# SBUF tiles of a four-layer network placed at multiples of 512 bytes

## The chip, the cores and the metric

The kernel runs on one core of a Trainium2 chip. A time is the device time of one execution in microseconds (us); what is compared is the median over several executions of a program. A profiled execution also leaves a trace, in which each instruction has its engine, its start and its duration. The core has five engines that work side by side: TensorE (PE, with its weight loads shown apart as PEld), VectorE (DVE), ScalarE (ACT), GpSimd (POOL) and SyncE (SP), whose queue starts most transfers. Operands lie in SBUF, the on-chip memory of 128 partitions; an address here is the number of bytes from the start of a partition, the same on every partition a tile uses.

## The reference

One sequence of 512 tokens with 1,024 features goes through four layers, all in float32: two of a first block, one of a second, one of a third. Each layer has a mixer and a feed-forward network with a hidden width of 2,816. What counts for the change is that every layer is a row of large products with weights from HBM, and that three mixers hold a running sum of log decays along the tokens, started anew at the first token of each chunk. Cut down:

```python
def first_block(x, c, ...):                     # layers 0 and 1, gated by a modulation silu(c) @ ada_w + ada_b
    x = x + gate * norm(mixer_ssd_mla(h(x)))    # layer 0: state-space scan (SSD) beside latent attention
    x = x + gate * norm(swiglu(h(x)))
    x = x + gate * norm(mixer_gla_nsa(h(x)))    # layer 1: gated linear attention beside sparse attention
    x = x + gate * norm(swiglu(h(x)))

def second_block(x, ...):                       # dilated attention, two convolution branches, feed-forward

def third_block(x, ...):                        # RWKV-7 beside gated DeltaNet, feed-forward
    u = rms_norm_3(x, norm1_g); p = u @ w_in
    ...
    h = causal_depthwise_conv_3(rms_norm_3(x, norm2_g) @ ffn_up, ffn_conv_w)
    x = x + (silu(h_gate) * h_up) @ ffn_down
    return rms_norm_3(x, final_g)

# the running sums of decays, within each chunk:
#   SSD:       a_cs = cumsum(dt * a)        over chunks of 128 tokens, 16 heads
#   GLA:       bc = cumsum(log_a)           over chunks of tokens, 4 heads of 128 features
#   DeltaNet:  gc = cumsum(g)               over chunks of tokens, 4 heads
```

## The kernel before

**Products.** Activations are kept by feature: a tile [128 features, 512 tokens], 2,048 bytes a partition. A float32 product is made in three passes of float32r parts: weights and activations are split into a high and a low part, and `mm3` (L246 on) issues high by high, high by low, low by high into one PSUM bank. Its two operands are the weights (128x128, the stationary tile: `whi` or `wlo`) and the activations (128x512, the moving tile: `h`, the input of a layer, or `s`, a slot of a phase). All of its matmuls are recorded at line L248. `gemm_tok` (L334) makes products by token the other way round: the activations are stationary, 128 tokens at a time, and up to 512 columns of weights move (L349 to L351).

**Weights.** `wtiles` (L222) takes at most 8 blocks of 128x128: one transfer of 512 KB on SyncE's queue into `wraw`, then `split` (L360) makes `whi` on ScalarE (L364) and `wlo` on VectorE (L365). A tile of 8 blocks serves 24 matmuls. A scheduler of priorities sets the order on each engine; what a mixer computes besides its products (small two-pass float32 matmuls at L824, L837, L844 among them) is traced with steps so that products fill the gaps between.

**Memory.** Four pools that last for the whole program are laid one behind the other in this order: `cpool` (constants `cst` and `vec`), `wpool` (`wraw`, `whi`, `wlo`), `tpool` (small tiles and temporaries `ta`, `tb`, `td`), `hpool` (eight slots of 4,096 bytes for `h`). Behind them lies a pool of the phase, with slots `s` of 4,096 bytes, which each phase opens anew. Each tile is rounded up to 32 bytes only, so the size of the constants decides where all others begin: `wraw`, `whi` and `wlo` start at 128 past a multiple of 512, the `h` slots at 320 past one, and so do the slots of all phases but one. In the mixer of block 3 (`b3_mixer`, L1656 on), two tiles of constants lie ahead of the slots, which puts these at 384.

**Running sums.** `rst128` is a constant of 512 columns in `cst`, 1 everywhere but at the first column of each 128. A scan computes, column by column, constant times the running value plus the next element, so one scan of 512 columns does four chunks of 128. There are six: one for layer 0 (L993 in `l0_ssd`, 16 partitions), four for layer 1 (L1315 in `gla_decays`, one for each head), one for block 3 (L1998 in `gdn_decays`, 4 partitions):

```python
nc.vector.tensor_tensor_scan(bs(hd), self.c("rst128"), e, 0.0, ALU.mult, ALU.add)
```

Of the kernel before, what the change touches and what calls it, by code (L numbers as in the profile page):

```python
# [26 lines left out]
# order of the work: priorities and steps between what runs side by side, slots and tiles of the phases  # L27
# [21 lines left out]
class Core:  # L49
    """Helpers shared by the layers: weight streaming, float32 products in three passes of float32r  # L50
    parts, norms over features. Activations by feature live in slots of 4 KB a partition."""

    def __init__(self, ctx, tc, a, offs):
# [4 lines left out]
        self.pp = pool("pp", space=PSUM)  # L58
        self.hslots = [None] * 8
# [19 lines left out]
    def consts(self, group, t=None, queue=None):  # L79
        """Load a group of constants, not before the instruction of self.mark has been issued."""  # L80
        if t is None:
            t = self.s4([128, self.a[group].shape[1]])
        if self.mark is None:
            (queue or self.nc.scalar).dma_start(t, self.a[group])
        else:
            with self.tc.issue_after(self.mark.ins):
                self.nc.scalar.dma_start(t, self.a[group])
        self.groups[group] = t
# [12 lines left out]
    # ---- memory: tiles of one tag are handed out in the order traced, so streams of work that are to  # L101
    # run side by side have tags of their own
    @contextmanager
    def psum(self, **banks):
        """The banks of the streams a and b, for the phases in the block."""
# [31 lines left out]
    def s4(self, shape=(128, 2, T), dt=F32, tag="s4"):  # L137
        """A slot of 4 KB a partition of the phase."""
        return self.spool.tile(list(shape), dt, tag=tag, name=self.nm(tag), bufs=self.nslots[tag] if isinstance(self.nslots, dict) else self.nslots)

    def fa(self, dt=F32, tag="s4"):
        """Tiles of features [128, T], two to a slot, taken when first used."""
# [11 lines left out]
    def h4(self, i, dt=F32):  # L154
        """Slot i % 8 (two tiles of features) of the memory of the input of a layer, free for float32, or for
        float32r parts, in place of those before."""
# [6 lines left out]
    def ha(self, slots, dt=F32):  # L163
        """As fa, in slots of the input of a layer."""
# [11 lines left out]
    def parts(self, tag="s4"):  # L176
        """Tiles of features as float32r parts: x(k) = (high, low). Tag h: the input of a layer."""
# [9 lines left out]
    def later(self, by):  # L187
        """What the block traces yields to what is traced up to `by` instructions after it."""
# [6 lines left out]
    def paced(self, by):  # L195
        """Products traced in the block, and what belongs to them, run between what is traced after it: a step
        of 3 passes every `by` instructions."""
# [10 lines left out]
    def beside(self):  # L208
        """What the block traces has the priority of what is traced after it."""
# [4 lines left out]
    def step(self, at):  # L214
        """The priority of one step of paced products, counted from at."""
# [6 lines left out]
    def wtiles(self, src, blocks):  # L222
        """At most 8 blocks [128, 128] of weights, as float32r parts [128, 1024]."""
# [12 lines left out]
    def wload(self, w, m0, nm, k0, nk):  # L236
        """m-tiles m0.. and k-tiles k0.. of a packed weight [m, 128, k, 128], as float32r parts: nm times a
        function of k."""
# [15 lines left out]
    def gemm(self, w, x, evac, m0=0, nm=None, wide=False, tail=0):  # L254
        """For each m-tile of packed w: evac(m, PSUM [128, T]) of w^T x; x(k) gives float32r parts, to be
        scaled by token after the product if there is x.rows. Wide: 4 m-tiles at first, for tiles of x that
        become ready one after the other, or 3 by halves of the tokens where x does. Tail: the last m-tiles
        by halves of the tokens, with evac(m, PSUM of the half, its slice)."""
# [22 lines left out]
    def gemm_tail(self, w, x, evac, m0, n):  # L281
        """At most 24 blocks of weights, loaded once. What follows the first half runs under the second."""
# [19 lines left out]
    def gemm_wide(self, w, x, evac, m0, n):  # L302
# [5 lines left out]
        for half in halves:  # L308
            for k in range(nk):
# [3 lines left out]
                for m in range(n):  # L313
                    # the first product of a bank clears it for both halves
# [19 lines left out]
    def gemm_tok(self, w, x, evac, n0=0, n=None):  # L334
        """By token: evac(j, PSUM [128, n]) of x^T w for the 4 tiles of tokens; w packed [128, k, N], n <= 512."""
# [24 lines left out]
    def split(self, hi, lo, src, scale=None):  # L360
        """hi + lo = src (times a per-partition scale), both float32r."""
# [10 lines left out]
    def sq_acc(self, acc, src, first, scale=1.0):  # L372
        """acc (+)= (src scale) squared."""
# [8 lines left out]
    def tok_sums(self, tiles, p=None, first=True, last=True):  # L382
        """[128, 4] by token in PSUM: sums over the partitions of all tiles. Not first: added to a bank with sums."""
# [6 lines left out]
    def pow_rstd(self, p, n, eps, pool=False):  # L390
        """(p / n + eps) ** -0.5 for a few columns p."""
# [8 lines left out]
        # Newton's method, from half the exponent: 3.5e-2, 2e-3, 5e-6, rounding  # L400
# [7 lines left out]
    def rstd_tok(self, tiles, n, eps=EPS, pool=False):  # L408
        """[128, 4] by token: (sum over partitions and tiles / n + eps) ** -0.5."""
        return self.pow_rstd(self.tok_sums(tiles), n, eps, pool)  # L410

    def bcast_tok(self, r):
        """[128, 4] by token -> PSUM [128, T], the same on every partition."""
        p = self.ps()
        self.bcast_to(p, r, 0)
        return p

    def bcast_to(self, p, r, j0):
        """[128, n] by token, of the tiles j0.. of tokens, into p."""
# [19 lines left out]
    def norm_h(self, r, x, gain, shift=None, update=None, h=None, half=slice(0, T)):  # L439
        """float32r parts of x rows gain (+ shift), by feature; r [128, T] the rows. update(k) completes x(k).  # L440
        With h: the half of the tokens of h."""
# [20 lines left out]
    def set_rows(self, h):  # L462
        """At the start of a phase: the factors by token that its input lacks, on all partitions."""
# [2068 lines left out]
```

## Time and profile before

| | us |
|---|---|
| median of 3 runs | 3778.25 |
| lowest and highest run | 3776.22, 3787.38 |
| span of the profiled execution | 3789.9 |
| TensorE busy in it | 3690.6 (97%) |
| weight loads (PEld, beside TensorE) | 2946.1 (78%) |
| VectorE busy | 2194.6 (58%) |
| ScalarE busy | 1357.0 (36%) |
| GpSimd busy | 242.3 (6%) |

The profiled execution is one of its own, with the time in the third line. A busy engine is one that has an instruction under way; matmuls are pipelined, so the duration of one overlaps the next, and the distance from one start to the next tells how fast they go. In a timeline a line of two instructions (x2) stands for both, with the start of the first and the end of the second. The granted clock (PEclk) is TensorE's clock as a share of 2.4 GHz, the upper of its two levels; 0.50 is the lower one, 1.2 GHz.

In order of time, the stages are: layer 0's mixer up to 471 us, its feed-forward to 841, layer 1's mixer to 1344, its feed-forward to 1714, block 2's mixer to 2384, its feed-forward to 2749, block 3's mixer to 3426, its feed-forward to 3761, and the last norm. "FFN" below means a feed-forward stretch.

### The profile page before, as it was taken

Reading aid. Unit: us, or ns where it says so; the run is one execution under the profiler, and the core shown is the slowest. Engines: PE = TensorE matmul, PEld = TensorE weight load, DVE = VectorE, ACT = ScalarE, POOL = GpSimd, SP = SyncE. Lnnn points to the kernel's source line nnn. Section 1 sums busy time; section 2 is a strip of 40 time slices with the busy share of each in tenths; the row PEclk is TensorE's granted clock in tenths of the full one; section 3 lists DMA queues with packets and bytes.
Section 4 is the critical chain, followed back from the end, with each engine's and each line's share of the span. In section 5 each row is a group of like instructions: output and inputs, shape, how many; then the busy total and the mean of one; then the engine's idle time right before and its main releaser. Section 6 shows DMA issues by size and latency. Waiting matters only on the chain.

```text
span 3789.9 us, 50851 instructions
## 1 busy us (share of the span) xinstructions
PE 3690.6 (97%) x20496; PEld 2946.1 (78%) x20496; DVE 2194.6 (58%) x3803; ACT 1357.0 (36%) x2197; POOL 242.3 (6%) x214
## 2 busy tenths in 40 slices
PE   7998999999999999999999999999999999999999
PEld 5776788877887778877878888788877777887887
DVE  7866655454377653338629354665466656766652
ACT  5344432324254432322332243443343332334432
POOL 2003100110022100101000010000000000100000
PEclk9998999999999999999989999999999999999999
DMA  6511265533310242333112234223321121152232
GB/s 217 181 47 56 99 201 188 167 111 98 119 31 23 66 152 94 117 95 103 57 39 73 84 102 138 90 95 116 93 98 40 61 69 43 32 178 89 95 117 73
DMA packets 120219, 373.75 MB, mean 99 GB/s; under 512 B 12064, under 2 KB 20128, under 8 KB 119984
## 3 DMA queue, kind: packets, MB, share of 16 engines
q1 hardware_dynamic: 105008, 322.05, 26.0%
q10 hardware_dynamic: 14976, 48.45, 3.8%
q8 instruction: 161, 2.64, 0.3%
q14 instruction: 74, 0.61, 0.1%
HBM read 349.49 MB, written 20.97 MB: 98 GB/s over the span
## 4 chain that ended last, share of the span: by engine, by line
PE 91%; DVE 6%; ACT 1%; issue 1%; DMA 0%; POOL 0%; POOLq 0%; DVEq 0%; ACTq 0%
PE pg L248 68%; PE pa L248 3%; PE pb L844 2%; PE pb L824 1%; PE pb L837 1%; PE pb L1264 1%; DVE wlo L365 1%; PE pa L387 1%; PE pg L1351 1%; PE pb L2264 1%; DVE wa L2142 1%; PE pg L349 0%; PE pa L349 0%; PE pa L350 0%; PE pg L350 0%
## 5 line engine op out<-in xcount | busy, mean ns | idle before, releaser
L248 PE MATMUL pg<-h,whi 128*128 128x512 f32 (+1 forms) x5584 | 1801.3, 401 | 44.8 <-ACT h L458 14.9
L248 PEld LDWEIGHTS pg<-h,whi 128*128 128x128 f32 x5584 | 1047.1, 190 | 307.3 <-ACT h L458 18.7
L248 PE MATMUL pg<-h,wlo 128*128 128x512 f32 (+1 forms) x2792 | 1113.4, 399 | 0.0
L364 ACT ACTIVATE whi<-wraw 128x1024 fp32r<-128x1024 f32 (+3 forms) x540 | 547.0, 1014 | 1414.7 <-PE pg L248 1106.1
L365 DVE TENSOR_TENSOR wlo<-wraw,whi 128x1024 fp32r<-128x1024 f32 (+3 forms) x540 | 639.2, 1185 | 665.2 <-ACT whi L364 662.4
L248 PE MATMUL pg<-s,whi 128*128 128x512 f32 (+1 forms) x2044 | 629.7, 390 | 2.6 <-DVE s L906 2.4
L248 PEld LDWEIGHTS pg<-h,wlo 128*128 128x128 f32 x2792 | 532.3, 191 | 123.5 <-issue 3.7
L248 PEld LDWEIGHTS pg<-s,whi 128*128 128x128 f32 x2044 | 379.1, 189 | 94.5 <-DVE s L906 3.7
L248 PE MATMUL pg<-s,wlo 128*128 128x512 f32 (+1 forms) x1022 | 397.3, 389 | 0.0
L248 PEld LDWEIGHTS pg<-s,wlo 128*128 128x128 f32 x1022 | 192.5, 188 | 43.5
L802 DVE SCALAR_TENSOR_TENSOR td<-td,vec,td 128x511 f32<-128x511 f32 (+1 forms) x188 | 139.9, 747 | 59.5 <-ACT td L798 57.9
L2142 DVE CUSTOM_DVE_ANT_0 wa<-wa,scb,vec 128x1024 f32<-128x1024 f32 x90 | 121.7, 1354 | 71.3 <-DMA wa<-in_l_ada_dram 71.2
L327 DVE TENSOR_TENSOR td<-pg,rows 128x512 f32<-128x512 f32 x130 | 89.7, 691 | 98.3 <-PE pg L248 98.0
L1500 DVE SCALAR_TENSOR_TENSOR s<-s,vec,s 128x504 f32<-128x504 f32 (+25 forms) x180 | 121.4, 731 | 0.4
L844 PEld LDWEIGHTS pb<-s,tb 128*128 128x128 f32 x600 | 83.6, 198 | 31.3 <-DVE tb L842 9.3
L248 PE MATMUL pa<-h,whi 128*128 128x512 f32 (+1 forms) x336 | 97.1, 363 | 0.0
L364 ACT ACTIVATE s<-td 128x512 fp32r<-128x512 f32 x94 | 59.3, 630 | 102.3 <-DVE td L489 102.0
L844 PE MATMUL pb<-s,tb 128*128 128x64 f32 x600 | 90.7, 281 | 2.9 <-DVE tb L842 2.9
L365 DVE TENSOR_TENSOR s<-td,s 128x512 fp32r<-128x512 f32 x94 | 66.9, 712 | 31.1 <-ACT s L364 31.1
L489 DVE TENSOR_TENSOR td<-td,pg 128x512 f32<-128x512 f32 x44 | 30.3, 688 | 80.9 <-PE pg L248 80.9
L248 PEld LDWEIGHTS pa<-h,whi 128*128 128x128 f32 x336 | 61.2, 194 | 10.1
L798 ACT ACTIVATE td<-td,vec 128x512 f32<-128x512 f32 x94 | 66.4, 708 | 4.5 <-DVE td L327 3.1
(804 smaller groups left out, 4140.4 us busy)
## 6 DMA issues: line engine op xcount, KB each, us to landing
wraw<-in_b_in_dram SPq DMA_DIRECT2D x112, 512.0 KB, 3.2
wraw<-in_l_up_dram SPq DMA_DIRECT2D x88, 512.0 KB, 3.2
wraw<-in_b_up_dram SPq DMA_DIRECT2D x88, 512.0 KB, 3.2
wa<-in_l_ada_dram ACTq DMA_DIRECT2D x80, 512.0 KB, 3.3
wraw<-in_l_in_dram SPq DMA_DIRECT2D x51, 512.0 KB, 3.3
wraw<-in_l_down_dram SPq DMA_DIRECT2D x32, 512.0 KB, 3.5
wraw<-in_b_down_dram SPq DMA_DIRECT2D x32, 512.0 KB, 3.5
xd<-s SPq DMA_DIRECT2D x28, 512.0 KB, 2.7
```

The lines of the kernel that those rows point to most:

```text
L248: mm = lambda *a, **k: self.nc.tensor.matmul(*a, **k, skip_group_check=True)
L327: self.nc.vector.tensor_mul(y, ps, rows)
L364: i = nc.scalar.activation(hi, src, AF.Copy)
L365: nc.vector.tensor_sub(lo, src, hi.bitcast(F32))
L387: self.pe_mark = self.nc.tensor.matmul(p[:, j : j + 1], t[:, j * 128 : j * 128 + 128], self.c("ones"), start=first and i + j == 0, stop=la ...
L798: nc.scalar.activation(out, ps, AF.Copy, scale=w(taps - 1))
L802: nc.vector.scalar_tensor_tensor(out[:, s:], ps[:, : T - s], w(taps - 1 - s), out[:, s:], ALU.mult, ALU.add)
L824: nc.tensor.matmul(s[:, :w], q, k, start=True, stop=True)
L837: nc.tensor.transpose(pt[:, b * 128 : b * 128 + 128], p[:, b * 128 : b * 128 + 128], self.ident)
L844: nc.tensor.matmul(o, st[:, b * 128 : b * 128 + 128], v(b), start=b == 0, stop=b == nb - 1)
L1500: nc.vector.scalar_tensor_tensor(out[:, s:], x[:, : T - s], tap(30 - s), out[:, s:], ALU.mult, ALU.add)
L2142: nc.vector.tensor_tensor_reduce(w, w, self.scb, 1.0, b, ALU.mult, ALU.add, o)
```

## The change

Two tiles that nothing reads are put at the ends of `cpool` and `tpool`, to fill the bytes up to the next multiple of 512. Each gets a memset of one column on GpSimd. To make room, `rst128` shrinks from 512 to 128 columns (`cst` from 788 to 404), and a scan of 512 columns becomes four of 128 in a new helper. In `b3_mixer` the two tiles of constants are rounded up to 128 columns, and a small tile grows from 80 to 128. Comments are dropped and line numbers shift by up to 11; all else is as it was.

```diff
+PADS = dict(cpool=384, tpool=320)
...
+        for n, size in PADS.items():
+            t = getattr(self, n).tile([128, size // 4], F32, name="pad")
+            nc.gpsimd.memset(t[:, :1], 0.0)
...
-    "rst128": _grid(lambda p, u: u % 128 != 0, 512),
+    "rst128": _grid(lambda p, u: u != 0, 128),
...
+    def scan128(self, out, x):
+
+        for t in (slice(c, c + 128) for c in range(0, T, 128)):
+            self.nc.vector.tensor_tensor_scan(out[:, t], self.c("rst128")[: x.shape[0]], x[:, t], 0.0, ALU.mult, ALU.add)
...
-        nc.vector.tensor_tensor_scan(cs, self.c("rst128")[:16], adt, 0.0, ALU.mult, ALU.add)
+        self.scan128(cs, adt)
...
-            nc.vector.tensor_tensor_scan(bs(hd), self.c("rst128"), e, 0.0, ALU.mult, ALU.add)
+            self.scan128(bs(hd), e)
...
         for g in ("cst3", "cst3b"):
-            self.consts(g, self.spool.tile([128, a[g].shape[1]], F32, name=g))
-        sm = self.small([128, 80], tag="b3", bufs=1)
+            n = a[g].shape[1]
+            self.consts(g, self.spool.tile([128, -(-n // 128) * 128], F32, name=g)[:, :n])
+        sm = self.small([128, 128], tag="b3", bufs=1)
...
-        nc.vector.tensor_tensor_scan(ab[:4], self.c("rst128")[:4], sp, 0.0, ALU.mult, ALU.add)
+        self.scan128(ab[:4], sp)
```

The start of each kind of tile, as bytes past a multiple of 512, in the two built programs:

| tile | before | after |
|---|---|---|
| `wraw`, `whi`, `wlo` | 128 | 0 |
| `h` slots | 320 | 0 |
| slots `s`, temporaries of a phase, block 3's mixer aside | 320 | 0 |
| slots `s` of block 3's mixer | 384 | 0 |

So the float32r matmuls with 512 columns come in these pairs of offsets (moving, stationary): before, 11,214 of (320, 128) at L248, 288 of (384, 128) at L248 in block 3, and 216 of (128, 320) in the product by token; after, all 11,718 of (0, 0).

On VectorE, before, the four scans of layer 1 stand right behind the operations that feed them (L1314); `s4_1159` and `s4_1164` are slots with two heads each, `ta` the temporaries, and a scan is printed as SCALAR_TENSOR_TENSOR:

```order
L1314 SCALAR_TENSOR_TENSOR ta_1158_6413<-s4_1159_6414,ta_1158_6413 128x512
L1314 SCALAR_TENSOR_TENSOR ta_1161_6420<-s4_1159_6414,ta_1161_6420 128x512
L1315 SCALAR_TENSOR_TENSOR s4_1159_6414<-cst_95,ta_1158_6413 128x512
L1315 SCALAR_TENSOR_TENSOR s4_1159_6414<-cst_95,ta_1161_6420 128x512
L1314 SCALAR_TENSOR_TENSOR ta_1163_6426<-s4_1164_6427,ta_1163_6426 128x512
```

And after, at the same place:

```order
L1324 SCALAR_TENSOR_TENSOR ta_1158_6420<-s4_1159_6421,ta_1158_6420 128x512
L1324 SCALAR_TENSOR_TENSOR ta_1161_6427<-s4_1159_6421,ta_1161_6427 128x512
L828 SCALAR_TENSOR_TENSOR s4_1159_6421<-cst_99,ta_1158_6420 128x128 x4
L828 SCALAR_TENSOR_TENSOR s4_1159_6421<-cst_99,ta_1161_6427 128x128 x4
L1324 SCALAR_TENSOR_TENSOR ta_1163_6433<-s4_1164_6434,ta_1163_6433 128x512
```

Each scan has become four in a row at its old place; nothing else has moved. At the start of GpSimd's queue, before, the memsets of the program's constants, the first of the kernel's own (`e`), and the first power of a norm:

```order
L2522 MEMSET const-bfloat16-1.0 128x1
L2522 MEMSET const-uint8-127 128x1
L2527 UNCONDITIONAL_BRANCH
L2226 MEMSET e_2641 128x8
L398 ISA
L398 TENSOR_TENSOR rya_131<-rxa_132,cst 128x4
```

And after:

```order
L2533 MEMSET const-bfloat16-1.0 128x1
L2533 MEMSET const-uint8-127 128x1
L2538 UNCONDITIONAL_BRANCH
L63 MEMSET pad 128x1 x2
L2237 MEMSET e_2648 128x8
L403 ISA
L403 TENSOR_TENSOR rya_135<-rxa_136,cst 128x4
```

The two memsets of the pads stand ahead of the kernel's first. On the other engines the rows are those of before but for a few neighbours of equal priority that change places.

## Rows read from the trace of the kernel before

**Rows 1.** Page, the chain that ended last, by engine and line; cores.

```profile
PE 91%; DVE 6%; ACT 1%; issue 1%; DMA 0%; POOL 0%; POOLq 0%; DVEq 0%; ACTq 0%
PE pg L248 68%; PE pa L248 3%; PE pb L844 2%; PE pb L824 1%; PE pb L837 1%; PE pb L1264 1%; DVE wlo L365 1%; PE pa L387 1%; PE pg L1351 1%; PE pb L2264 1%; DVE wa L2142 1%; PE pg L349 0%; PE pa L349 0%; PE pa L350 0%; PE pg L350 0%
...
core 0: 3789.9 us, clock 0.979
```

**Rows 2.** Groups by shape, TensorE: busy us, mean ns; idle before, releasers.

```profile
L248 PE MATMUL pg<-h,whi 128*128 128x512 f32 x5392 | 1763.3, 405 | 38.4 <-ACT h L458 11.7 <-DVE h L459 8.9 <-DVE td L327 5.9
L248 PE MATMUL pg<-h,wlo 128*128 128x512 f32 x2696 | 1087.1, 403 | 0.0
L248 PE MATMUL pg<-s,whi 128*128 128x512 f32 x1924 | 608.2, 397 | 2.6 <-DVE s L906 2.4 <-DVE s L802 0.2
L248 PE MATMUL pg<-s,wlo 128*128 128x512 f32 x962 | 380.7, 396 | 0.0
```

**Rows 3.** Timeline of TensorE, moving tile h: start, us, what.

```profile
3031.28 0.63 PE L248 MATMUL pg<-h,whi 128*128 128x512 f32 x2
3031.74 0.40 PE L248 MATMUL pg<-h,wlo 128*128 128x512 f32 x1
...
3035.48 0.63 PE L248 MATMUL pg<-h,whi 128*128 128x512 f32 x2
```

**Rows 4.** Timeline of TensorE, moving tile s of block 3.

```profile
3383.99 0.61 PE L248 MATMUL pg<-s,whi 128*128 128x512 f32 x2
3384.45 0.39 PE L248 MATMUL pg<-s,wlo 128*128 128x512 f32 x1
...
3388.07 0.61 PE L248 MATMUL pg<-s,whi 128*128 128x512 f32 x2
```

**Rows 5.** Timeline of TensorE, product by token.

```profile
980.41 0.39 PE L349 MATMUL pg<-whi,h 128*128 128x512 f32 x1
...
985.91 0.39 PE L349 MATMUL pg<-whi,h 128*128 128x512 f32 x1
```

**Rows 6.** Chain in 1891 to 1921, then that window's row.

```profile
1894.03 1.28 PE pg L248 x3
...
1891.00:1921.00 30.00, 30.00 (x88) 22.02 (x88) 4.62 (x25) 10.89 (x41) 0.00 (x0) 0.50 0.05 17
```

**Rows 7.** Windows: span, busy PE PEld DVE ACT POOL, PEclk, DMA share, GB/s.

```profile
128.00:471.00 343.00, 320.86 (x1761) 249.94 (x1759) 236.07 (x440) 144.14 (x270) 53.42 (x43) 0.94 0.27 89
471.00:841.00 370.00, 363.25 (x1545) 288.90 (x1545) 195.38 (x253) 112.15 (x147) 17.90 (x13) 0.99 0.51 166
...
1714.00:2384.00 670.00, 670.00 (x2955) 541.80 (x2956) 373.79 (x594) 219.71 (x404) 33.75 (x19) 0.96 0.26 85
...
2749.00:3426.00 677.00, 673.22 (x6340) 527.31 (x6339) 426.47 (x958) 226.47 (x381) 11.86 (x17) 0.99 0.23 74
```

**Rows 8.** Groups by shape, VectorE: whole span, 2384:2749, 2749:3426.

```profile
L365 DVE TENSOR_TENSOR wlo<-wraw,whi 128x1024 fp32r<-128x1024 f32 x460 | 570.2, 1241 | 571.0 <-ACT whi L364 568.4 <-PE pg L248 0.5 <-ACT sb L1803 0.4
...
L489 DVE TENSOR_TENSOR td<-td,td 128x512 f32<-128x512 f32 x22 | 15.1, 687 | 0.0
...
L2121 DVE TENSOR_TENSOR s<-s,s 128x512 f32<-128x512 f32 x4 | 2.7, 685 | 0.0
```

**Rows 9.** Chain at 96.91; line L1315; timeline at 14.93.

```profile
96.91 1.16 DVE s L993
...
L1315 DVE TENSOR_TENSOR_SCAN s<-cst,ta x4: 1200/1210/1220, 922.6 to 927.2; 128x512 f32<-128x512 f32 x4
...
14.93 0.16 DVE L396 TENSOR_SCALAR rxa<-pa 128x4 f32<-128x4 f32 x1 [1.96 <-PE pa L387]
```

**Rows 10.** Timeline of the first 20 us.

```profile
0.73 0.10 POOL L2226 MEMSET e<- 128x8 f32 x1 [0.29 <-POOLq L2522]
...
7.58 3.57 PE L387 MATMUL pa<-cst,sq 128*128 128x1 f32 x16 [7.58 <-DVE sq L2177]
...
15.17 1.01 POOL L398 TENSOR_TENSOR rya<-rxa,cst 128x4 f32<-128x4 f32 x1 [14.34 <-DVE rxa L396]
```

## The prediction

> **What bounds the kernel now.** The first view is the chain of work that ended last. TensorE holds 91% of it, and a single line, L248 (the three passes of a float32r product in `mm3`), holds 68% with the tile `pg` and 3% with `pa` [rows 1]. So the question is what one such matmul takes, not what anybody waits for. The groups by shape give the count: the four largest groups of L248 with 512 columns hold 5392 + 2696 + 1924 + 962 = 10,974 matmuls [rows 2]. Their mean duration there (about 400 ns) overlaps the next one and is no price; the price is the distance from one start to the next, and the timeline shows that.
>
> In block 3, where the moving tile is `h`, six triples start between 3031.28 and 3035.48: 4.20 us for 18 matmuls, 233.3 ns each [rows 3]. In the same block, the same line with weights at the same place but with the moving tile in a slot `s` has six triples between 3383.99 and 3388.07: 4.08 us, 226.7 ns each [rows 4]. What differs is the place in SBUF: `h` lies at 320 past a multiple of 512 bytes, that slot at 384; both tiles hold 2,048 bytes a partition, and the weights lie at 128 in both cases. Every other phase has its slots at 320, as `h`.
>
> The third kind is the product by token (L349 to L351), where the weights move (at 128) and `h` is stationary (at 320): eight triples from 980.41 to 985.91, 24 matmuls of 229.2 ns [rows 5]. So a moving tile at a multiple of 128 bytes is faster than one that is 64 past it, and what it is paired with counts as well. Last, at the lower of the two clock levels three L248 matmuls take 1.28 us, 426.7 ns each, in a stretch with a granted clock of 0.50 [rows 6]. That is 512 columns at 1.2 GHz with nothing on top, though the offsets are the same. At 2.4 GHz the columns alone would be half of it, 213.3 ns. So the 13.4 to 20 ns above that belong to something that does not speed up with the array and hides behind it at the lower clock; the reading of the operands fits.
>
> **The change, part by part.** *The offsets.* After it every float32r matmul with 512 columns has both operands at a multiple of 512. No row shows such a matmul, so I bound it. One end is 233.3 ns, as `h` now [rows 3]: no change. The other is 213.3 ns, the columns alone [rows 6]. Between them the nearest row is 226.7 ns [rows 4], where the moving tile is at a multiple of 128 but not of 512, and the weights are not either. Going from 64 to 128 was worth 6.7 ns; from 128 to 512 are two more doublings, for the moving tile and for the weights. I take one more step of the same size, 220 ns, because it stays as near to the row as one step allows and lies halfway to the floor: 13.3 ns a matmul.
>
> In an FFN stretch TensorE is busy for 363 of 370 us while VectorE is at about half [rows 7]; there are four such stretches with about 6,000 of the matmuls in all. There they follow each other and nothing else sets the time, so all counts: 6,000 x 13.3 = 80 us. The weights arrive in tiles for 24 matmuls, 5.6 us apart now and 5.3 then; VectorE needs 1.24 us for such a tile [rows 8] and the DMA engines are half busy [rows 7], so neither becomes late. The other 5,000 matmuls lie in the mixers. The mean granted clock of 0.979 [rows 1] tells that 4.2% of the span ran at the lower level, nearly all of it in the mixers, without gain there: about 7% of their time. 5,000 x 13.3 x 0.93 = 62 us. In the mixers the products also fill waits in dependent work (VectorE is busy for 374 of 670 and 426 of 677 us, and TensorE nearly throughout [rows 7]); a filler that ends earlier uncovers part of these waits. I take 80%, 50 us, with 60% and 100% as bounds. Together 130 us.
>
> By the Trainium skill ("TensorE: Matmul & The Clock Gate", section "Wait — 56ns, not 53.3ns?") warm back-to-back matmuls start N / 2.4 GHz plus about 2.5 ns apart, an estimate of 215.8 ns for 512 columns. No row here comes near it at 2.4 GHz; the matmuls that open that page are bf16, these have four bytes an element. By it the sum would be 105 us in the FFNs and about 60 in the mixers, and the time about 3,613.
>
> *VectorE and ScalarE* get the same offsets. For VectorE it should not matter: a 128x512 operation on two SBUF tiles takes 687 ns at 320 and 685 ns at 384 [rows 8]. ScalarE is taken to behave alike; it is not on the chain's list beyond 1% [rows 1]. The small two-pass float32 products (L844, L824, L837 with 1 to 2% of the chain each [rows 1]) are left at nothing; many of their operands stay off the multiples of 512.
>
> *The scans.* Six scans of 512 columns become 24 of 128. One takes 1.16 us on the chain, the others 1.2 us each beside products [rows 9]. A quarter of the columns costs a quarter, and each of the 18 added instructions adds at most what an operation on four columns takes, 0.16 us [rows 9]: 2.9 us if all of them were on the path, and nothing if none is. On the chain I find the three of layer 0: I take 0.3.
>
> *The constants.* `cst` shrinks from 788 to 404 columns. TensorE's first work at 7.58 waits for VectorE, not for a landing [rows 10]: nothing, and a few tenths of a microsecond at most if the smaller transfer lets the inputs land sooner. *The pads* are two memsets of one column at the start of GpSimd's queue, 0.10 us for the like of them, and GpSimd then idles until 15.17 [rows 10]: nothing; without that idle time 0.2 us.
>
> The sum is -130 us against the profiled span of 3789.9: 3,660. The median of the runs is 3778.25, 11.65 below that span, so the forecast for the median is **3,648 us**, 3.4% faster.
>
> **The rivals.** *128 bytes are all that counts.* Then `h` behaves as the slots of block 3 do now, 226.7 ns. For: that is the only faster value that a row of L248 shows. Against: [rows 5], where 128 for the moving tile alone gives 229.2. 6.7 ns: 40 us in the FFNs and 85% of 31 in the mixers, 66 in all: 3,712.
>
> *The floor is reached.* 213.3 ns, 20 ns a matmul: 120 us and 70% of 93, because more waits are uncovered: 185 in all, 3,593. For: with a step for each doubling it would come out so. It shares the forecast's case, whose ends are then 3,575 and 3,675.
>
> *The offset is not the cause.* The 6.7 ns between [rows 3] and [rows 4] could belong to the tile or to the moment. Then all stays: 3,778. Against: line, weights' offset and phase are the same. The Trainium skill ("SBUF — State Buffer", section "Specifications (TRN2)") gives lines of 16 bytes and a penalty for each crossing to a new one; every tile in question starts at a multiple of 64 already, so by that rule nothing would change. The trace differs, 233.3 against 226.7 ns, and the trace decides.
>
> *Slower: equal offsets collide.* [Rows 5] against [rows 4] says that the two streams of a matmul may disturb each other: both moving tiles are at a multiple of 128, yet the pairs differ by 2.5 ns. The change puts moving tile and weights on the same offset. One more step of 6.7 ns, 240 ns: 10,974 x 6.7 x 0.96 = 70 us, 3,848. It decides from about 1 ns above 233.3 on, which is 0.3% of the time. Against: offsets that differ by 256 (128 and 384) and by 192 (128 and 320) show no trend of that kind, since the 192 apart gives both 229.2 and 233.3.
>
> *The wait moves.* TensorE gets faster, and the split of the weights, their transfer or the dependent work of the mixers becomes late; half of the gain goes: 3,713. For: VectorE is busy for 236 of 343 us in layer 0's mixer [rows 7]. Against: elsewhere it has room.
>
> **How the numbers follow.** The forecast's case (213 to 222 ns) gets 0.55, 128 bytes alone 0.26, the moved wait 0.06, no effect 0.07, slower 0.06. A measurement of this kernel can tell 0.3% (11 us) from no change. Faster by more: 0.55 + 0.26 + 0.06 = 0.87; within: 0.07; slower: 0.06. The range goes from 3,575 (the floor with 90% of the mixers) to 3,725 (226.7 ns with 60% of the mixers, and a few microseconds for scans); it leaves out the last two cases.
>
> **What would show it.** In the profile after, L248 triples in the timeline should start 0.66 us apart (0.64 for the floor, 0.68 for the 128-byte rival, 0.70 for no effect, more for the collision), alike for `s` and `h`. An FFN stretch should be 19 to 21 us shorter. VectorE's 128x512 rows should stay at about 687 ns. TensorE's idle time should grow by some 12 us, in the mixers; if it grows by 50 or more, the 80% was too high. The forecast is wrong if the triples do not come below 0.68, or if they do and the FFN stretches do not follow.

## The result, and the profile after

The changed kernel takes 3738.06 us (median of 4 runs, 3729.26 to 3744.64) against 3779.59 for the kernel before in the same comparison; the ratio is 0.9888, with a 95% interval of 0.987 to 0.9907. It is faster by 41.5 us or 1.1%, where 3.4% were forecast, and lies 13 us above the range. The profiled execution has this span and mean granted clock (0.979 before, [rows 1]):

```profile
core 0: 3739.4 us, clock 0.975
```

The chain that ended last, by engine and by line; L253 is L248 of before:

```profile
PE 91%; DVE 6%; ACT 1%; issue 1%; DMA 0%; POOL 0%; POOLq 0%; DVEq 0%; ACTq 0%
PE pg L253 67%; PE pa L253 3%; PE pb L854 2%; PE pb L834 1%; PE pb L847 1%; PE pb L1274 1%; DVE wlo L370 1%; PE pa L392 1%; PE pg L1361 1%; PE pb L2275 1%; PE pg L354 1%; PE pa L354 1%; PE pa L355 1%; PE pg L356 1%; PE pg L355 1%
```

The chain has kept its shape, so the question stays what one matmul takes. The timeline of TensorE in layer 0's feed-forward (start, duration, what):

```profile
560.67 0.61 PE L253 MATMUL pg<-h,whi 128*128 128x512 f32 x2
561.12 0.39 PE L253 MATMUL pg<-h,wlo 128*128 128x512 f32 x1
...
563.39 0.61 PE L253 MATMUL pg<-h,whi 128*128 128x512 f32 x2
```

Four triples in 2.72 us are 226.7 ns a matmul: not the 220 of the forecast, but the value that [rows 4] showed for the slots of block 3. Over all saturated matmuls (start to start below 260 ns; 11,009 before, 10,992 after) the mean went from 233.1 to 227.1 ns.

TensorE's instructions come in the same order in both programs, so the 20,496 matmuls of one trace can be laid beside those of the other, and each distance from one start to the next be put to a kind:

| kind of distance | before, us | after, us | change |
|---|---|---|---|
| 512 columns, saturated | 2565.9 | 2496.8 | -69.1 |
| 512 columns at the lower clock level | 75.8 | 78.8 | +3.0 |
| 512 columns, longer distances | 235.5 | 243.9 | +8.4 |
| 256 columns | 166.6 | 169.3 | +2.7 |
| small float32 products and transposes | 731.5 | 737.1 | +5.6 |
| first to last matmul | 3775.3 | 3725.9 | -49.4 |

By stage the four feed-forward stretches are 10.7, 10.0, 8.1 and 9.0 us shorter, 37.8 in all, with 41.1 us less in their saturated matmuls; all else, with 28.0 us less in its saturated matmuls, brings 11.6. Here are layer 0's feed-forward and the mixers of blocks 2 and 3 by windows (columns as in [rows 7]):

```profile
465.30:824.70 359.40, 352.02 (x1546) 287.29 (x1547) 196.09 (x254) 112.20 (x146) 18.40 (x13) 1.00 0.53 171
...
1684.30:2348.90 664.60, 663.92 (x2955) 546.73 (x2954) 371.95 (x593) 220.24 (x404) 33.34 (x19) 0.95 0.26 86
...
2705.90:3385.30 679.40, 675.37 (x6339) 532.76 (x6338) 426.64 (x961) 226.63 (x381) 11.84 (x17) 0.98 0.23 74
```

The first answers the second line of [rows 7]. The other two show granted clocks of 0.95 and 0.98, where block 2 had 0.96 and block 3 0.99 before: some of the gain there went into time at the lower clock level. VectorE's 128x512 operation takes 685 ns (687 in [rows 8]), and a scan of 128 columns about 0.4 us. First the groups of VectorE in block 2's feed-forward (busy us, mean ns):

```profile
L494 DVE TENSOR_TENSOR td<-td,td 128x512 f32<-128x512 f32 x22 | 15.1, 685 | 0.0
```

The view of line L828 (durations in ns, least, median and most):

```profile
L828 DVE TENSOR_TENSOR_SCAN s<-cst,ta x20: 385/401/418, 96.9 to 911.1; 128x128 f32<-128x128 f32 x16, 16x128 f32<-16x128 f32 x4
```

And the chain (start, us, what):

```profile
96.94 1.35 DVE s L828 x4
```

That is layer 0's scan: 1.35 us for four, 1.16 for one before [rows 9]; the forecast's 0.3 was 0.19.

### The profile page after: what moved, and what is told of

The parts are those of the page before. It is cut to its first block, busy times and chain, and to the rows that moved or that the text cites. A ratio compares the mean times of both kernels' runs of the same rounds, so it can differ in the third digit from the quotient of the medians.

```text
span 3739.4 us, 50867 instructions
## 1 busy us (share of the span) xinstructions
PE 3637.7 (97%) x20496; PEld 2956.0 (79%) x20496; DVE 2192.0 (59%) x3821; ACT 1357.4 (36%) x2197; POOL 242.1 (6%) x216
## 4 chain that ended last, share of the span: by engine, by line
PE 91%; DVE 6%; ACT 1%; issue 1%; DMA 0%; POOL 0%; POOLq 0%; DVEq 0%; ACTq 0%
PE pg L253 67%; PE pa L253 3%; PE pb L854 2%; PE pb L834 1%; PE pb L847 1%; PE pb L1274 1%; DVE wlo L370 1%; PE pa L392 1%; PE pg L1361 1%; PE pb L2275 1%; PE pg L354 1%; PE pa L354 1%; PE pa L355 1%; PE pg L356 1%; PE pg L355 1%
## 5 line engine op out<-in xcount | busy, mean ns | idle before, releaser
L253 PE MATMUL pg<-h,whi 128*128 128x512 f32 (+1 forms) x5584 | 1776.2, 397 | 45.4 <-ACT h L463 14.4
L253 PEld LDWEIGHTS pg<-h,whi 128*128 128x128 f32 x5584 | 1049.1, 191 | 278.2 <-issue 18.7
L253 PE MATMUL pg<-h,wlo 128*128 128x512 f32 (+1 forms) x2792 | 1101.2, 395 | 0.0
L253 PE MATMUL pg<-s,whi 128*128 128x512 f32 (+1 forms) x2044 | 620.5, 386 | 3.4 <-DVE s L916 2.8
L253 PEld LDWEIGHTS pg<-h,wlo 128*128 128x128 f32 x2792 | 533.5, 191 | 109.7 <-issue 4.2
L253 PEld LDWEIGHTS pg<-s,whi 128*128 128x128 f32 x2044 | 379.9, 189 | 84.1 <-DVE s L916 3.2
L253 PE MATMUL pg<-s,wlo 128*128 128x512 f32 (+1 forms) x1022 | 392.7, 384 | 0.0
L253 PEld LDWEIGHTS pg<-s,wlo 128*128 128x128 f32 x1022 | 192.9, 189 | 38.0
L253 PE MATMUL pa<-h,whi 128*128 128x512 f32 (+1 forms) x336 | 95.8, 359 | 0.0
L494 DVE TENSOR_TENSOR td<-td,pg 128x512 f32<-128x512 f32 x44 | 30.2, 687 | 75.9 <-PE pg L253 75.8
L253 PEld LDWEIGHTS pa<-h,whi 128*128 128x128 f32 x336 | 61.2, 194 | 8.9 <-issue 0.2
```

Source lines behind the costliest of these rows:

```text
L253: mm = lambda *a, **k: self.nc.tensor.matmul(*a, **k, skip_group_check=True)
```

## The experiments

**What decides the price of a matmul.** Theory A was that only the moving tile's place counts, modulo 128 bytes; theory B that the pair counts; theory C that multiples of 512 bytes count. A kernel of matmuls alone measured all pairs, and three variants of the two kernels undid one part each.

`sweep`, 24 matmuls in a row for each pair:

```python
for k in range(8):
    x, w = slice((k % 2) * 512, (k % 2) * 512 + n), slice((k % 4) * 128, (k % 4) * 128 + 128)
    mm(p, wh[:, w], xh[:, x], ...); mm(p, wh[:, w], xl[:, x], ...); mm(p, wl[:, w], xh[:, x], ...)
```

> A kernel of its own that holds only float32r matmuls, 24 in a row for each of the 64 pairs of a moving tile at 0, 64, ... 448 past a multiple of 512 bytes (tiles xa to xh) and weights at 0, 64, ... 448 (wa to wh); its output is only a copy of the last product. Theory A, the place of the moving tile counts and only modulo 128: 226.7 ns from start to start in the rows xa, xc, xe, xg, 233.3 ns in xb, xd, xf, xh, whatever the weights. Theory B, the pair counts: the rows differ within one moving tile by the weights; (128, 320) gives the 229.2 ns of the product by token, and (0, 0) need not be the best. Theory C, 512 bytes count: xa is below xc, xe, xg. With 256 columns, A expects the same difference in bytes, half of it (3.3 ns), in favour of the multiples of 128; the traces of the two kernels show the reverse, 115.2 ns at (320, 128) and 119.7 at (0, 0), which B allows.

Its timeline, for a moving tile at 320 with weights at 0, at 128, and at 320 (`xf` with `wa`, `wc`, `wf`; first and last of 24):

```profile
279.05 0.39 PE L43 MATMUL pga<-xfh,wah 128*128 128x512 f32 x1
...
284.32 0.39 PE L43 MATMUL pga<-xfh,wal 128*128 128x512 f32 x1
...
290.01 0.40 PE L43 MATMUL pga<-xfh,wch 128*128 128x512 f32 x1
...
295.38 0.39 PE L43 MATMUL pga<-xfh,wcl 128*128 128x512 f32 x1
...
306.69 0.39 PE L43 MATMUL pgb<-xfh,wfh 128*128 128x512 f32 x1
...
311.92 0.39 PE L43 MATMUL pgb<-xfh,wfl 128*128 128x512 f32 x1
```

Divided by 23: 229.1, 233.5 and 227.4 ns. The whole table of 64 pairs comes down to the distance from the moving tile to the weights (address of the weights less that of the moving tile) modulo 256; the means of start-to-start distances over both kernels of matmuls, by it, moving tiles at odd and at even multiples of 64 alike:

| weights less moving, modulo 256 | 0 | 64 | 128 | 192 |
|---|---|---|---|---|
| ns a matmul of 512 columns | 227.4 | 233.4 | 232.3 | 229.3 |

(0, 0) is left out there, since both kernels of matmuls begin with it, partly at the lower clock; at the full clock it took 226.7 ns in each, and 227.1 in the changed kernel. So B holds; A and C fall.

`w128` and `h320`, the changed kernel with the weights, or the moving tiles, back at their old places; `scans`, the kernel before with its scans cut in four:

```diff
-PADS = dict(cpool=384, tpool=320)
+PADS = dict(cpool=512, tpool=192)      # w128
+PADS = dict(cpool=384, tpool=128)      # h320
...
-        nc.vector.tensor_tensor_scan(cs, self.c("rst128")[:16], adt, 0.0, ALU.mult, ALU.add)
+        self.scan128(cs, adt)          # scans: at all three places, rst128 still 512 wide
```

> The changed kernel with the moving tiles at 0 as there, but the weights at 128 past a multiple of 512, as before the change. Theory A (only the moving tile's place modulo 128 counts): triples 0.68 us apart, the same time as the changed kernel, 3,738 us within 8. Theory B (the pair counts): half of the gain at most comes from the moving tile; between 229 and 231 ns a matmul, 3,752 to 3,762 us.

> The changed kernel with the weights at 0 as there, but the moving tiles (h and the slots) at 320, as before the change. Theory A: triples 0.70 us apart and the time of the kernel before, 3,780 us within 8. Theory B: below 232 ns a matmul and 3,755 to 3,770 us.

> The kernel before with its 6 scans of 512 columns cut into 24 of 128, and nothing else: every tile where it was. By the prediction's own step: 0.3 us, at most 2.9, 3,778 to 3,783 us, and a scan of 128 columns takes 0.3 to 0.46 us. Rival (the scans give back what is missing of the gain): 10 us or more, 3,790 us.

`w128` took 3798.83 us (ratio 1.0032, 1.0012 to 1.0053), `h320` 3760.23 (0.9928, 0.99 to 0.9956), `scans` 3785.25 (1.002, 0.9998 to 1.0043). Their saturated matmuls take 232.9, 229.2 and 233.1 ns in the mean, within 0.6 ns of the table's values for distances of 128, 192 and 64. Eight triples of `w128` in layer 0's feed-forward take 5.60 us, 233.3 ns a matmul:

```profile
600.60 0.63 PE L253 MATMUL pg<-h,whi 128*128 128x512 f32 x2
...
606.20 0.63 PE L253 MATMUL pg<-h,whi 128*128 128x512 f32 x2
```

Four triples of `h320` take 2.75 us, 229.2 ns a matmul:

```profile
599.77 0.62 PE L253 MATMUL pg<-h,whi 128*128 128x512 f32 x2
...
602.52 0.62 PE L253 MATMUL pg<-h,whi 128*128 128x512 f32 x2
```

`w128` is slower than both theories had it: putting the moving tiles alone on multiples of 512 gains nothing to speak of, and putting the weights alone there gains two thirds of the whole. (Its time above the kernel before is a matter of the clock; see the table further down.)

**Is 512 needed?** `eq320` puts both on 320, `apart256` puts them on 384 and 128; `after2` is the changed kernel beside them, and `sweep2` a second kernel of matmuls, with other counts of columns and types:

```diff
-PADS = dict(cpool=384, tpool=320)
+PADS = dict(cpool=192, tpool=320)      # eq320
+PADS = dict(cpool=512, tpool=64)       # apart256
```

> The changed kernel once more, beside the others on one chip. The profiles say that its 512-column matmuls start 5.9 ns earlier each (233.1 to 227.1), 65 us for 11,000 of them, and that its TensorE ran 24 us longer at the lower clock level than that of the kernel before (187 against 164 us). Theory D, the clock differs from execution to execution by chance: over many executions both kernels have the same mean granted clock (0.982 within 0.002), and the changed one is 55 to 62 us faster, about 3,722. Theory E, the change itself lowers the clock: its mean granted clock stays 0.003 or more below that of the kernel before, and it is 40 to 48 us faster, about 3,737.

> The changed kernel with all moving tiles and all weights at 320 past a multiple of 512 bytes in place of 0. Theory B, sharpened by the table of pairs (the distance from moving tile to weights modulo 256 counts, 0 is best): 227 ns as the changed kernel; and since 256 columns took 113.4 ns in the table with the moving tile at 320 and 119.5 at 0, 840 matmuls x 6 ns = 5 us less: 3 to 6 us faster than the changed kernel at equal granted clock. Theory C (multiples of 512 bytes count): slower than the changed kernel, 230 ns or more, 30 us or more.

> The changed kernel with the moving tiles at 384 and the weights at 128 past a multiple of 512. Theory B: 227 ns, since the distance is 256; the time of the changed kernel within 5 us at equal granted clock. Theory C: slower by 30 us or more. A multiple of 256 in each address counting by itself would give the price of (0, 128) and (128, 0), 232 to 233 ns, and 3,790 us or more.

> A second kernel of matmuls alone: moving tile at 0 and at 320, weights at four distances (0, 64, 128, 192 modulo 256), 512 down to 128 columns, then weights of 64 columns, distances of 16, 32 and 48, plain float32 and bfloat16 operands. Theory B expects at 512 columns 227, 233.4, 232.3 and 229.3 ns for distances of 0, 64, 128 and 192 for both moving tiles. If the price is a fixed loss for each matmul, it is the same at every count of columns until the weight load sets the pace; if it is one for each byte moved, it shrinks in proportion. Open: whether two-byte and plain float32 operands show it at all (if they do, their differences by distance exceed 2 ns).

They took 3738.98 (`after2`; 0.9875, 0.9848 to 0.9902), 3738.58 (`eq320`; 0.9865, 0.9833 to 0.9896) and 3740.10 us (`apart256`; 0.9882, 0.9851 to 0.9913), all with 227.1 ns in the mean. The timeline of `eq320`, in layer 0's feed-forward, has four triples in 2.72 us as the changed kernel:

```profile
599.67 0.62 PE L253 MATMUL pg<-h,whi 128*128 128x512 f32 x2
600.12 0.39 PE L253 MATMUL pg<-h,wlo 128*128 128x512 f32 x1
...
602.39 0.62 PE L253 MATMUL pg<-h,whi 128*128 128x512 f32 x2
```

Any distance of a multiple of 256 does. The 3 to 6 us that `eq320` was to gain on the 256-column matmuls did not come: these take 119.7 ns there as in the changed kernel, 115.2 before. The expectation had read the table's row for 320 where the weights were at 128 and 256 (113.4 ns); at a distance of 0 `sweep2` has 120.2.

`sweep2` shows that the law belongs to 512 columns of float32r. Its timeline for 448 columns, moving tile at 0, weights at 0 and at 192 (first and last of 24):

```profile
201.70 0.37 PE L52 MATMUL pga<-xah,wah 128*128 128x448 f32 x1
...
206.46 0.36 PE L52 MATMUL pga<-xah,wal 128*128 128x448 f32 x1
...
216.39 0.36 PE L52 MATMUL pgb<-xah,wdh 128*128 128x448 f32 x1
...
220.99 0.36 PE L52 MATMUL pgb<-xah,wdl 128*128 128x448 f32 x1
```

That is 206.7 ns (from the starts in ns) at a distance of 0, the worst of the four there (202.2, 203.9 and 200.0 at 64, 128 and 192). With 384 columns the four are 174.4, 176.7, 176.1 and 173.5; with 320 all are 146.6, and with 128 and 192 columns all 110 to 112. Matmuls in bfloat16 took 215.8 ns at every distance, plain float32 429.1 to 429.2 for each recorded one. So it is no fixed loss that goes with a bad distance, nor one for each byte.

**Where the rest went.** Every execution has its mean granted clock on record. Within a program, a mean clock that is lower by 0.001 goes with 2.55 us more (a line fitted inside 16 sets of executions, 169 in all; single executions scatter about it by 2 us). The offsets are those of most of a kernel's matmuls. Read at the same clock, the kernels stand like this:

| kernel | moving, weights | distance | ns a matmul | executions | mean clock | mean us | at a clock of 0.980 |
|---|---|---|---|---|---|---|---|
| before | 320, 128 | 64 | 233.1 | 66 | 0.9821 | 3783.0 | 3788.4 |
| `sameoff` | 320, 128 | 64 | 233.3 | 12 | 0.9820 | 3785.1 | 3790.2 |
| `scans` | 320, 128 | 64 | 233.1 | 12 | 0.9792 | 3791.8 | 3789.7 |
| `w128` | 0, 128 | 128 | 232.9 | 12 | 0.9767 | 3795.2 | 3786.7 |
| `h320` | 320, 0 | 192 | 229.2 | 6 | 0.9773 | 3756.2 | 3749.4 |
| changed | 0, 0 | 0 | 227.1 | 10 | 0.9762 | 3738.6 | 3728.9 |
| `eq320` | 320, 320 | 0 | 227.1 | 6 | 0.9767 | 3736.7 | 3728.2 |
| `apart256` | 384, 128 | 0 | 227.1 | 6 | 0.9748 | 3742.0 | 3728.8 |
| `min64` | 384, 128 | 0 | 227.2 | 8 | 0.9837 | 3717.1 | 3726.6 |

At equal clock the change is worth 59 us, which is about what 11,000 matmuls of 6.0 ns (66) leave after 4 us lost on the 256-column ones. Some 15 us of that (0.006 of clock) are missing in the executions because the changed kernel ran at a mean clock of 0.976 and the kernel before at 0.982. Whether this belongs to the change was the next question; `after2`, with 3,739 us at a clock of 0.976, came out about as theory E had it, in which the change lowers the clock. `before2` is the kernel before once more; `sameoff` keeps all of the change but the offsets; `min64` is the least change that sets the distance to 256; `bump` moves the start of block 2's mixer in the changed kernel by 1.8 us.

```diff
-PADS = dict(cpool=384, tpool=320)
+PADS = dict(cpool=512)                                          # sameoff: no pad behind the small tiles
...
+        nc.gpsimd.memset(self.tpool.tile([128, 16], F32, name="pad")[:, :1], 0.0)   # min64, on the kernel before
-    "rst128": _grid(lambda p, u: u % 128 != 0, 512),
+    "rst128": _grid(lambda p, u: u % 128 != 0, 384),
+        for t in (slice(0, 384), slice(384, 512)):               # each scan in two
...
+        for _ in range(getattr(self, "bump", 0) if first else 0):   # bump, in mm3; 8 ahead of block 2's first
+            mm(ps, wh, xh, start=True, stop=False)
```

> The kernel before, unchanged, once more. It is here for its profile and clocks: in the first profile of it TensorE ran 47 us at the lower clock level in block 2's mixer, in those of all other kernels 54 to 87. Theory D (the clock falls by chance at a few places of the program): its profiles differ among themselves as they differ from the others; a granted clock of 0.976 goes with some 75 us at the lower level in block 2's mixer. Theory E (the change lowers the clock): never over 60 us there.

> The changed kernel with the offsets of the kernel before: moving tiles at 320, weights at 128, everything else of the change kept (small constants, scans of 128, pads). Theory B: 233.3 ns again and at equal granted clock the time of the kernel before within 4 us. Theory E1 (the lower clock comes with the other parts of the change and not with faster matmuls): mean granted clock 0.976 to 0.978 and about 3,800 us. E2 (it comes with faster matmuls): mean clock 0.981 to 0.983 as the kernel before and about 3,783 us.

> The kernel before with one pad of 64 bytes ahead of the small tiles: moving tiles at 384, weights at 128, distance 256; the room comes from a constant of 384 columns in place of 512, which cuts each of the 6 scans in two; block 3's own slots come to lie at 448. Theory B: 227 ns for all but those 288 (229.3), and at equal granted clock the time of the changed kernel within 4 us; median 3,735 to 3,742 us if the clock falls as there, 3,722 if it stays as in the kernel before. Theory C (multiples of 512): 3,770 us or more.

> The changed kernel with the first matmul of block 2's mixer issued eight times more (1.8 us of TensorE), which moves all that follows by 1.8 us and changes nothing else. Theory D: where the clock falls in block 2's and 3's mixers shifts, comes or goes with the moment, by 10 us or more at the lower level against the 67 and 31 us that three profiles of the changed layout agree in. Rival (the work alone decides): the same falls at the same matmuls within 3.4 us, and a time 1.8 us above the changed kernel's.

`before2` took 3781.26 us, `sameoff` 3781.38 (1.0006, 0.9988 to 1.0024), `min64` 3717.11 (0.982, 0.9799 to 0.9842), `bump` 3736.26 (0.987, 0.9845 to 0.9895). `sameoff` settles the other parts of the change: without the offsets it is worth nothing, and its clock is that of the kernel before (E1 falls). `min64` has the fast matmuls and the higher clock (E2 falls as well). And the second profile of the kernel before differs from the first as kernels differ from each other: block 2's mixer took 657.9 us in it, 669.7 in the first. In the profile of `bump` TensorE ran at the lower level for 44 us in block 2's mixer and 7 in block 3's (twice the missing share of the granted clock, times the stretch), where the changed kernel has 67 and 31: the fall moved with the work, as theory D had it.

The time sits in two stretches of block 2's attention, 100 to 107 matmuls each, most of them small ones. The second stretch by windows (columns as in [rows 7]), in the changed kernel:

```profile
1929.20:1961.90 32.70, 32.70 (x106) 24.06 (x106) 5.80 (x27) 11.75 (x43) 0.00 (x0) 0.53 0.05 17
```

In `before2`:

```profile
1948.10:1971.40 23.30, 23.30 (x107) 16.87 (x107) 5.87 (x27) 11.28 (x43) 0.00 (x0) 1.00 0.08 24
```

In `min64`:

```profile
1923.10:1946.40 23.30, 23.30 (x107) 16.88 (x107) 5.82 (x27) 11.26 (x43) 0.00 (x0) 1.00 0.07 24
```

And in `apart256`:

```profile
1924.40:1958.40 34.00, 34.00 (x106) 24.90 (x106) 6.37 (x28) 11.72 (x43) 0.00 (x0) 0.50 0.05 16
```

The same work takes 33 to 34 us at a granted clock of 0.50 to 0.53 and 23.3 at 1.00, without an idle moment of TensorE in any of them. Ahead of it, between the two stretches, the clock was full in all four. From the start of block 2's mixer up to the first of the two stretches, `apart256` and `min64` run alike within 0.1 us (their matmul number 8,900 starts 180.0 us after number 8,057 in both), and yet the clock falls in one and not in the other. So nothing that was found in the trace decides it. If it is the moment at which the same work meets the clock's control, moving the work must move the fall. That was tried from both sides: `min64b` repeats the good one, `min64bump` moves it by the 1.8 us of `bump`, `bump4` and `bump12` move the changed kernel by 0.9 and 2.7 us.

```diff
-        self.bump = 8
+        self.bump = 4          # bump4; 12 in bump12; 8 on top of min64 in min64bump
```

> The kernel with one pad of 64 bytes once more. Theory P (the moment decides where the clock falls): it has executions with a granted clock of 0.976 to 0.979 too, 3,730 to 3,740 us, though most are as its first four, 3,717. Theory L (layout and parts decide): all at 0.984 and 3,713 to 3,718 us.

> The kernel with one pad of 64 bytes, with the first matmul of block 2's mixer issued eight times more (1.8 us). Theory P: the mean granted clock falls by 0.003 or more and the time rises by 10 us or more, by far more than the 1.8 us. Theory L: 0.984, and 1.8 us more.

> The changed kernel with the first matmul of block 2's mixer issued four times more (0.9 us). Theory P: another mean granted clock than the 0.976 of the changed kernel in this or in the one moved by 2.7 us, up to 0.984, and then 3,717 to 3,725 us. Theory L: 0.976 and 3,739 us.

> The same with twelve times more (2.7 us). Theory P as for four times. Theory L: 0.976 and 3,741 us.

| kernel | median us | ratio | clock of its executions | at a clock of 0.980 |
|---|---|---|---|---|
| `min64b` | 3716.18 | 0.9827 (0.9813 to 0.9841) | 0.982 to 0.984 | 3726.1 |
| `min64bump` | 3746.38 | 0.99 (0.9885 to 0.9914) | 0.972 to 0.975 | 3728.6 |
| `bump4` | 3742.43 | 0.9889 (0.9874 to 0.9905) | 0.973 to 0.977 | 3727.2 |
| `bump` | 3736.26 | 0.987 (0.9845 to 0.9895) | 0.974 to 0.983 | 3729.5 |
| `bump12` | 3723.49 | 0.9846 (0.9831 to 0.986) | 0.976 to 0.983 | 3729.3 |

Eight matmuls more, 1.8 us of work, make `min64` 30 us slower, and twelve more make the changed kernel 15 us faster, while all five agree within 3.4 us at equal clock. The same two stretches in `min64bump`:

```profile
1857.00:1890.90 33.90, 33.90 (x101) 25.03 (x101) 5.07 (x29) 12.44 (x48) 0.00 (x0) 0.53 0.07 26
1932.50:1966.20 33.70, 33.70 (x106) 24.71 (x106) 5.34 (x28) 11.95 (x46) 0.00 (x0) 0.54 0.06 19
```

So the lower clock is no price of the layout: theory L falls, and moving the work moves the clock, as theory P had it. The added matmuls as such are not it, since eight of them lower the clock of `min64` and twelve raise that of the changed kernel. But P is not proven by this. It expected some executions of `min64b` at 0.976 to 0.979, and none of the four came below 0.982; and what the control of the clock responds to was not seen in any trace. (The Trainium skill, "TensorE: Matmul & The Clock Gate", section "Part 1: The HAM clock gate (the "warmup" mystery)", says that the window of the control runs freely and is not started by the kernel. The spread of one program, 0.972 to 0.986 over 66 executions of the kernel before, fits that; that all eight of `min64` lie at 0.982 or more and all four of `min64bump` at 0.975 or less does not follow from it.) What keeps the executions of one program on the same side stays open. `min64` is the fastest kernel of the study, by 21 us against the changed one in the median; at equal clock only 2 us of that are left, and the others go with the clock.

## Why the prediction was wrong

**TensorE as the bound: right.** The chain kept its shares, and in the feed-forward stretches nearly all that the matmuls gave came through: 5,938 saturated ones, 41.1 us less in them, 37.8 us shorter.

**The 13.3 ns a matmul: wrong, and this is the step that failed.** They gave 6.0. The prediction took the gain for steps by the power of two that divides the address, and "one more step of the same size" from 128 to 512 carried it to 220 ns. There is no such step: what counts is the distance of the two operands modulo 256. The rows held a first trace of it. [Rows 3] is (320, 128): the weights lie 192 behind, 64 modulo 256, 233.3 ns. [Rows 4] is (384, 128): 256 behind, 0 modulo 256, 226.7. [Rows 5] is (128, 320): 192 ahead, 229.2. The prediction looked at the distances and dropped their sign: "the 192 apart gives both 229.2 and 233.3", it said, and put the pair aside, though +192 and -192 are different distances modulo 256. With the sign, three rows and three values are three distances with a price each. That a distance of 256 counts as 0 no row showed; `sweep` did. By it the change is a move from 64 to 0, which [rows 4] had priced: 6.7 ns.

With 6.0 ns in its own sum (6,000 x 6.0 in the feed-forward stretches, 80% of 5,000 x 6.0 x 0.93 in the mixers) the forecast would have been about 3,720 us, still inside its range. What carried the result past the range's end of 3,725 came on top: some 15 us by the lower clock of those executions and 4 us by the 256-column matmuls.

**The mixers' 80%: not what happened.** The 20% were to go to uncovered waits; TensorE's idle time grew by 2.4 us (99.3 to 101.7, span less busy time) and not by some 12. At equal clock nearly all of the gain came through, 59 of 62 us. What took a part of it in the executions was a thing that the prediction held fixed: it carried the profile's 0.979 over to the kernel after, as 7% of the mixers without gain. The clock of one and the same program ranges from 0.972 to 0.986 here, 36 us by the fitted line, three times the 11 us that were taken as the bound of what can be told apart.

**The 256-column matmuls** were not in the sum. 840 of them went from 115.2 to 119.7 ns, 4 us the other way: the distance that suits 512 columns does not suit 256.

**The rest held.** Constants, pads and rounding: nothing (`sameoff`). Scans: 1.3 us at equal clock in `scans`, inside 0.3 to 2.9, though hardly more than the fitted line can tell. VectorE: unchanged. TensorE's first work began at 7.30 in place of 7.58, waiting for VectorE as before.

**The rivals.** "128 bytes are all that counts" named the right number, 226.7 ns, and gave 3,712, which the changed kernel would near only at the clock of `min64` (some 3,719 at 0.984, by the fitted line); its reason is wrong, since (0, 128) has both at multiples of 128 and takes 232.9. "Equal offsets collide" has it the wrong way round at 512 columns, where equal is best, and would have been right at 448, where equal is worst. The floor is not reached: no pair of offsets took less than 226.7 ns in the mean with float32r matmuls of 512 columns. The 215.8 ns that the prediction worked out from the Trainium skill ("TensorE: Matmul & The Clock Gate", section "Wait — 56ns, not 53.3ns?") are what bfloat16 showed (215.8) and float32r did not (226.7 at best). The lines of 16 bytes of the Trainium skill ("SBUF — State Buffer", section "Specifications (TRN2)") tell nothing of a pair of operands; here tiles that all start at multiples of 64 differ by up to 6.7 ns a matmul.

## What to carry to other kernels

Where float32r matmuls of 512 columns follow each other, read the address of the weights less that of the moving tile, modulo 256, and set it to 0: here one pad of 64 bytes did all that aligning everything to 512 did. Other counts of columns want another distance (448 and 256 did here), so count the matmuls of each kind first. Keep the sign when you compare offsets, and lay all rows that you have into one table before you choose a variable. And before a gain or a loss of half a per cent is put to a change, compare the mean granted clocks of the executions, and shift the same work by a microsecond or two to see whether it stays.

## What the runs showed of the hardware

The best distance depends on the count of columns: 0 at 512 (227.4 ns against 233.4 at 64), 192 at 448 (200.0 against 206.7 at 0), none at 320 (146.6). With fewer columns in the weights it gets no faster: 64 columns of weights take 228 to 233 ns for 512 moving columns, 32 take 231 to 232. What in the memory or in the weight load makes these four values was not found; the runs give the law and not its cause. Offsets that are not multiples of 64 are no better: a moving tile that starts 4 bytes past a multiple of 512 took 235 to 237 ns, one at 16, 32 or 48 bytes 232 to 234. Weights at 16, 32 or 48 past one took 232 to 233.4, but for one pair: a moving tile at 320 with weights at 48, a distance of 240, took 227.6.

At the lower clock level all this vanishes: the median of a matmul of 512 columns there is 427 ns in every kernel, whether its distance is 0, 64, 128 or 192.
